# Diagonal blocks of the delta rule by SBUF transfers instead of ACT copies, with the first transpositions and clearings queued behind the last multiplication on DVE

## The chip, the cores and the metric

The kernel runs on one core of a Trainium2 chip. The core has engines that run their own instruction queues in order: PE (TensorE, matrix products; PEld is its weight load), DVE (VectorE), ACT (ScalarE), POOL (GpSimd) and SP (SyncE, which here only issues DMA transfers). The metric is the device time of one execution in microseconds (us), as the median of several executions.

## The reference

One encoder layer in float32 over 1024 tokens of width 1024. Two mixers read the same normalised input through one projection:

```python
xn   = _rmsnorm(h, norm_mix_w[l])
proj = xn @ w_in[l]
q_a, k_a, v_a, qkv_g, z_g, a_g, b_g = jnp.split(proj, SPLIT_POINTS, axis=-1)
attn = _windowed_gqa(...)          # 8 heads, window of 128
gdn  = _gdn_mixer(qkv_g, z_g, ...) # 4 heads of 128, both directions
h = h + jnp.concatenate([attn, gdn], axis=-1) @ w_out[l]
h = h + jnp.square(jax.nn.relu(_rmsnorm(h, norm_ffn_w[l]) @ w_ffn_in[l])) @ w_ffn_out[l]
```

The second mixer is a gated delta rule. In each chunk of tokens it needs the inverse of a unit triangular matrix:

```python
kk    = jnp.einsum("bnhcd,bnhsd->bnhcs", k, k)
a_mat = jnp.where(strict, beta[..., :, None] * kk * decay, 0.0)
t_mat = lax.linalg.triangular_solve(eye + a_mat, eye, left_side=True, lower=True)
```

The change touches only how the small diagonal blocks of `a_mat` are brought together before they are inverted.

## The kernel before

Large products are made in three passes of float32 parts: ACT rounds a weight tile (`split`, L123), POOL subtracts to get the rest (L124), and PE multiplies (L136 to L138 in `mm3`). The rounded weights live in three buffers with the tag `wh`, the rests in three of the tag `wl`, so the two instructions for the next weights can run as soon as PE has released a buffer. Results land in PSUM: four banks have the tag `psA` (the projections), four the tag `psB` (all else).

The stage of the change weaves two streams. The first is the rest of the input projection: v (`proj_conv`), the gate z (`proj_z`, whose results ACT takes out of PSUM with L473) and the attention's keys, values and queries (`proj_attn`, whose results DVE takes out with L491 and L509). The second belongs to the delta rule:

- `prep` loops over 8 chunks of 128 tokens, and in each over the 2 directions. PE makes k by k (`gg`, L646), k by q (`kq`, L648) and the rows of the decay with its mask (`rows`, L653 and L654); ACT takes the exponentials (L658, one for each of 4 heads); DVE multiplies to `at` (L662) and, as the last step, `dec` by `kq` (L670). `at` and `dec` are stored to device memory (L669, L671). ACT copies the four 32x32 diagonal blocks of each head out of `at` into `diag[d]` (L667).
- `eliminate` transposes `diag[d]` in blocks of 32x32 on DVE (L679, once for each direction), clears the result `t` on POOL (L680, L681) and then inverts all 256 blocks at once on DVE, in 31 steps of two instructions (L688, L690), each of which needs the one before.
- `diag_blocks` transposes the inverses back (L699, L700), and `invert` makes the 128x128 inverses from them on PE. It loads `at` again for two chunks (L721, into the buffers of `eliminate`), and begins with the products of L738, followed by L749 and L753.

Who goes first on each engine is set at build time by a scheduler that runs through the program with estimated times; the hardware then follows each queue strictly. `tc.issue_after(i)` puts the instructions of its block, where they are on the engine of instruction `i`, behind `i` in that engine's queue. The heads of v are transposed on PE into `psB` (L424) and multiplied out of it by DVE (L464). SP's queue holds the loads of weights (L254), the stores of `at`, `dec`, z (L474) and v (L465), and the loads of L721. Each transfer names one of eight counters in turn and waits until the eighth transfer before it has landed.

Of the kernel before, what the change touches and what calls it, by code (L numbers as in the profile page):

```python
# [14 lines left out]
ALU = mybir.AluOpType  # L15
# [3 lines left out]
SEQ = 1024  # L19
# [59 lines left out]
class Block:  # L79
# [397 lines left out]
    def proj_attn(self):  # L477


        nc = self.nc  # L480
        w = self.io["w_in"][0]
        raws = self.load_w(self.w_cols(w, C_AK, 256))
        lo, up = slice(0, 64), slice(64, 128)
        self.kh, self.kl = [self.pg(dt=F32R) for _ in range(2)], [self.pg(dt=F32R) for _ in range(2)]
        for v, o in enumerate((up, lo)):
            nc.vector.tensor_copy(out=self.kl[v][o, :], in_=self.zero[o, :].to_broadcast([64, SEQ]))
        self.va = self.pg((P, NT, P))
        for i, half, ps in self.pair(raws):
            tok = slice(half * HALF, (half + 1) * HALF)
            t = self.pt()  # L490
            nc.vector.tensor_copy(out=t, in_=ps)  # L491
            if i == 0:
                swap = self.pt()
                nc.sync.dma_start(out=swap[up, :], in_=t[lo, :])
                nc.sync.dma_start(out=swap[lo, :], in_=t[up, :])
                for v, (r, o) in enumerate(((lo, up), (up, lo))):
                    nc.scalar.copy(out=self.kh[v][r, tok], in_=t[r, :])
                    nc.scalar.copy(out=self.kh[v][o, tok], in_=swap[o, :])
                    nc.gpsimd.tensor_tensor(out=self.kl[v][r, tok], in0=t[r, :], in1=self.kh[v][r, tok].bitcast(F32),
                                            op=ALU.subtract)  # L500
            else:
                pv = self.transposed(t, 0)
                nc.vector.tensor_copy(out=self.va[:, 4 * half:4 * half + 4, :], in_=pv)
            yield 5.2
        for kv in range(2):
            raws = self.load_w(self.w_cols(w, C_AQ + 256 * kv, 256))
            for i, half, ps in self.pair(raws):
                q, qh = self.pt(), self.pt(dt=F32R)
                nc.vector.tensor_scalar(out=q, in0=ps, scalar1=0.125, scalar2=None, op0=ALU.mult)  # L509
                nc.scalar.copy(out=qh, in_=q)  # L510
                nc.gpsimd.tensor_tensor(out=q, in0=q, in1=qh.bitcast(F32), op=ALU.subtract)
                for part, t in enumerate((qh.bitcast(F32), q)):
                    nc.sync.dma_start(out=self.qad[kv, part, i, :, half * HALF:(half + 1) * HALF], in_=t)
                if i == 1 and half == 0:
                    self.qs.append(self.query(0, kv))
                yield 5.2
# [122 lines left out]
    def prep(self):  # L639
        nc = self.nc  # L640
        self.diag = [self.pg((P, 32, 32)) for _ in range(2)]
        for c in range(NT):
            sl = slice(c * P, (c + 1) * P)
            gg, kq = self.ps("psB", (P, GH, P)), self.ps("psB", (P, GH, P))
            for h in range(GH):
                nc.tensor.matmul(gg[:, h, :], self.kT[h][:, sl], self.kT[h][:, sl], start=True, stop=True)  # L646
            for h in range(GH):
                nc.tensor.matmul(kq[:, h, :], self.kT[h][:, sl], self.qT[h][:, sl], start=True, stop=True)  # L648
            for d in range(2):
                dec, at = self.pt((P, GH, P)), self.pt((P, GH, P))  # L650
                rows = self.ps("psB", (P, GH, P))
                i = 2 * c + d
                nc.tensor.matmul(rows, self.selb[:, i:i + 1].to_broadcast([P, P]), self.grow, start=True, stop=False)  # L653
                nc.tensor.matmul(rows, self.identb, self.maskb[d].unsqueeze(1).to_broadcast([P, GH, P]),  # L654
                                 start=False, stop=True)
                for h in range(GH):
                    i = 4 * d + h
                    nc.scalar.activation(out=dec[:, h, :], in_=rows[:, h, :], func=AF.Exp,  # L658
                                         bias=self.ngc[:, c, i:i + 1])
                for h in range(GH):  # L660
                    i = 4 * d + h
                    nc.vector.scalar_tensor_tensor(out=at[:, h, :], in0=dec[:, h, :],  # L662
                                                   scalar=self.cc[:, c, i:i + 1], in1=gg[:, h, :],
                                                   op0=ALU.mult, op1=ALU.mult)
                for q in range(4):
                    r = slice(32 * q, 32 * q + 32)
                    nc.scalar.copy(out=self.diag[d][r, :, 4 * c:4 * c + 4].rearrange("p i h -> p h i"),  # L667
                                   in_=at[r, :, r])
                nc.sync.dma_start(out=self.atd[c, :, d], in_=at)  # L669
                nc.vector.tensor_tensor(out=dec, in0=dec, in1=kq, op=ALU.mult)  # L670
                nc.sync.dma_start(out=self.pd[c, :, d], in_=dec)  # L671
                yield 1.5

    def eliminate(self):

        nc = self.nc
        m, t = self.dbl((P, 2, 32, 32)), self.dbl((P, 2, 32, 32))
        for d in range(2):
            nc.vector.transpose(out=m[:, d].rearrange("p a b -> p b a") if d else m[:, d], in_=self.diag[d])  # L679
        nc.gpsimd.memset(t.rearrange("p d a b -> p (d a b)"), 0.0)  # L680
        nc.gpsimd.memset(t.rearrange("p d a b -> p d (a b)")[:, :, 0:1024:33], 1.0)  # L681
        elim = self.pt((P, 2 * 256))
        yield 1.1
        for k in range(31):
            rr, xx = slice(k + 1, 32), slice(0, k + 1)
            nr, nx = 31 - k, k + 1
            tmp = elim[:, :2 * nr * nx].rearrange("p (d a b) -> p d a b", d=2, a=nr)
            nc.vector.tensor_tensor(out=tmp, in0=m[:, :, rr, k:k + 1].to_broadcast([P, 2, nr, nx]),  # L688
                                    in1=t[:, :, k:k + 1, xx].to_broadcast([P, 2, nr, nx]), op=ALU.mult)
            nc.vector.tensor_tensor(out=t[:, :, rr, xx], in0=t[:, :, rr, xx], in1=tmp, op=ALU.subtract)  # L690
            yield 0.8
        self.tdiag = t
# [745 lines left out]
```

## Time and profile before

| what | value |
|---|---|
| median of 3 runs | 1218.68 us (1217.45 to 1218.98) |
| the profiled execution's own time | 1218.1 us |
| its span, first to last instruction | 1216.4 us |
| mean granted clock of TensorE | 0.99 |
| the stage of the change, `prep` to the first product of `invert` | 147 to 270 us |
| ACT's copies L667 in it | 64, 26.8 us |

The profile is of one execution. A row of a timeline gives start, duration, engine, line and operation, output and inputs by the program's names, a count, and in brackets the idle time before it with what ended it. "SPq" is SP's own queue; its durations include waits between merged instructions. The tables by windows give the busy time of PE, PEld, DVE, ACT and POOL, then the granted clock (1.00 is full speed), the share of the DMA engines and GB/s.

### The profile page before, as it was taken

What the parts mean: (1) busy time and instruction counts of PE and PEld (TensorE: products, weight loads), DVE (VectorE), ACT (ScalarE), POOL (GpSimd) and SP (SyncE); (2) the same over time, 40 slices, a digit from 0 to 9 for tenths busy, and PEclk for the clock granted to TensorE, in tenths of its full rate; (3) what the DMA queues carried; (4) which work ended last, traced back from release to release, by engine and by line L of the source; (5) the groups of instructions that cost most, each with busy time, mean ns of one, the idle gap of its engine ahead of it and who ended that gap; (6) DMA issues with size and microseconds to landing.
All of it is one profiled execution on the core that took longest, in us unless ns stands there. A gap on an engine that the chain in (4) does not pass through costs nothing. (4 is left out here: it accounts for less than half of the span.)

```text
span 1216.4 us, 18458 instructions
## 1 busy us (share of the span) xinstructions
PE 1172.0 (96%) x6482; PEld 960.5 (79%) x6482; DVE 855.4 (70%) x1482; ACT 610.8 (50%) x1331; POOL 559.8 (46%) x470
## 2 busy tenths in 40 slices
PE   6999999899979999999999999999999999999996
PEld 5788878687768778888788888888878888888875
DVE  4676667994489996687854445454599796987976
ACT  6455597425385762134755454454645444334443
POOL 5354211234421224143855453544546565555694
PEclk9999999899989999999999999999999999999999
DMA  6124344433635667323153444444779535443323
GB/s 246 48 95 146 93 163 165 165 130 112 206 122 184 187 212 265 126 91 122 54 176 121 160 149 156 140 153 140 251 278 327 183 104 177 135 156 104 104 87 139
DMA packets 121630, 187.62 MB, mean 154 GB/s; under 512 B 11044, under 2 KB 64417, under 8 KB 121538
## 3 DMA queue, kind: packets, MB, share of 16 engines
q1 hardware_dynamic: 103876, 155.20, 38.7%
q10 hardware_dynamic: 17661, 31.24, 6.8%
q8 instruction: 51, 0.84, 0.3%
q14 instruction: 42, 0.34, 0.1%
HBM read 122.39 MB, written 63.49 MB: 153 GB/s over the span
## 5 line engine op out<-in xcount | busy, mean ns | idle before, releaser
L136 PE MATMUL psA<-pg,wh 128*128 128x512 f32 x416 | 165.2, 398 | 2.1 <-ACT pt L473 2.1
L138 PE MATMUL psA<-pg,wl 128*128 128x512 f32 x416 | 164.5, 395 | 0.0
L137 PE MATMUL psA<-pg,wh 128*128 128x512 f32 x416 | 164.2, 395 | 0.0
L124 POOL TENSOR_TENSOR wl<-wr,wh 128x512 fp32r<-128x512 f32 x44 | 66.3, 1529 | 156.8 <-ACT wh L123 129.0
L1207 DVE TENSOR_TENSOR pg<-pg 128x512 fp32r<-128x512 f32 x112 | 125.1, 1151 | 12.1 <-ACT pg L1206 12.1
L124 POOL TENSOR_TENSOR wh<-wr,wh 128x512 fp32r<-128x512 f32 x32 | 47.6, 1507 | 139.5 <-ACT wh L123 139.5
L1124 ACT ACTIVATE pt<-pt 128x512 f32<-128x512 f32 x64 | 40.4, 632 | 119.2 <-DVE pt L1114 114.7
L137 PE MATMUL psA<-pg,pg 128*128 128x512 f32 x256 | 99.6, 391 | 0.3 <-POOL pg L124 0.2
L136 PE MATMUL psA<-pg,pg 128*128 128x512 f32 x256 | 98.7, 390 | 0.9 <-DVE pg L1252 0.9
L138 PE MATMUL psA<-pg,pg 128*128 128x512 f32 x256 | 99.2, 389 | 0.0
L136 PEld LDWEIGHTS psA<-pg,wh 128*128 128x128 f32 x416 | 78.8, 189 | 19.5 <-ACT pt L473 2.4
L137 PEld LDWEIGHTS psA<-pg,wh 128*128 128x128 f32 x416 | 78.9, 190 | 18.0 <-issue 0.9
L138 PEld LDWEIGHTS psA<-pg,wl 128*128 128x128 f32 x416 | 78.8, 189 | 16.8
L124 POOL TENSOR_TENSOR pg<-wr,pg 128x512 fp32r<-128x512 f32 x48 | 73.7, 1567 | 39.3 <-ACT pg L123 39.3
L1206 ACT CAST pg<-pg 128x512 fp32r<-128x512 f32 x112 | 66.9, 620 | 37.6 <-DMA pg<-sd 27.8
L137 PE MATMUL psB<-pg,pg 128*128 128x512 f32 x192 | 74.9, 390 | 0.8 <-POOL pg L124 0.7
L138 PE MATMUL psB<-pg,pg 128*128 128x512 f32 x192 | 74.7, 389 | 0.0
L136 PE MATMUL psB<-pg,pg 128*128 128x512 f32 x192 | 74.7, 389 | 0.0
L123 ACT CAST wh<-wr 128x512 fp32r<-128x512 f32 x76 | 43.6, 623 | 52.7 <-PE psA L137 32.0
L1114 DVE TENSOR_TENSOR pt<-psB,pt 128x512 f32<-128x512 f32 x39 | 26.9, 689 | 58.8 <-PE psB L138 40.1
L1114 DVE TENSOR_TENSOR pt<-psA,pt 128x512 f32<-128x512 f32 x39 | 26.8, 688 | 52.6 <-PE psA L138 35.2
L136 PEld LDWEIGHTS psA<-pg,pg 128*128 128x128 f32 x256 | 48.0, 188 | 12.3 <-DVE pg L1252 2.2
(395 smaller groups left out, 3231.4 us busy)
## 6 DMA issues: line engine op xcount, KB each, us to landing
sd<-pt ACTq DMA_DIRECT2D x112, 256.0 KB, 2.0
pg<-sd SPq DMA_DIRECT2D x112, 256.0 KB, 2.9
wr<-in_w_ffn_in SPq DMA_DIRECT2D x32, 512.0 KB, 3.6
wr<-in_w_in SPq DMA_DIRECT2D x22, 512.0 KB, 3.9
pg<-in_x SPq DMA_DIRECT2D x16, 512.0 KB, 5.0
wr<-in_w_ffn_out SPq DMA_DIRECT2D x16, 512.0 KB, 4.6
sc<-kvd SPq DMA_DIRECT2D x14, 512.0 KB, 4.7
kvd<-pt SPq DMA_DIRECT2D x16, 256.0 KB, 2.4
```

What stands on the lines that cost most here:

```text
L123: a = nc.scalar.copy(out=h, in_=raw)
L124: b = (eng or nc.gpsimd).tensor_tensor(out=l, in0=raw, in1=h.bitcast(F32), op=ALU.subtract)
L136: nc.tensor.matmul(ps, wh, xh, start=first, stop=False, skip_group_check=onto)
L137: nc.tensor.matmul(ps, wh, xl, start=False, stop=False, skip_group_check=onto)
L138: return nc.tensor.matmul(ps, wl, xh, start=False, stop=last, skip_group_check=onto)
L1114: self.nc.vector.tensor_tensor(out=out, in0=in0, in1=in1, op=ALU.add)
L1124: self.nc.scalar.activation(out=c, in_=c, func=AF.Relu)
L1206: nc.scalar.copy(out=s[:, 0], in_=raw)
L1207: v.tensor_tensor(out=s[:, 1], in0=raw, in1=s[:, 0].bitcast(F32), op=ALU.subtract)
```

## The change

Three things. The four ACT copies for each chunk and direction become four DMA transfers from `at` to `diag[d]` within SBUF, issued by SP behind the store of `at`; each moves 32 partitions with four pieces of 128 bytes. `diag[d]` is now laid out with the blocks outside and the columns inside, so that a piece is contiguous, and the transpositions read it with a stride. Last, the two transpositions, and two clearings of `proj_attn` that also run on DVE (L486), are queued behind the last L670.

```diff
@@ proj_attn
-        for v, o in enumerate((up, lo)):
-            nc.vector.tensor_copy(out=self.kl[v][o, :], in_=self.zero[o, :].to_broadcast([64, SEQ]))
+        with self.tc.issue_after(self.decayed):
+            for v, o in enumerate((up, lo)):
+                nc.vector.tensor_copy(out=self.kl[v][o, :], in_=self.zero[o, :].to_broadcast([64, SEQ]))
@@ prep
+                nc.sync.dma_start(out=self.atd[c, :, d], in_=at)
                 for q in range(4):
                     r = slice(32 * q, 32 * q + 32)
-                    nc.scalar.copy(out=self.diag[d][r, :, 4 * c:4 * c + 4].rearrange("p i h -> p h i"),
-                                   in_=at[r, :, r])
-                nc.sync.dma_start(out=self.atd[c, :, d], in_=at)
-                nc.vector.tensor_tensor(out=dec, in0=dec, in1=kq, op=ALU.mult)
+                    nc.sync.dma_start(out=self.diag[d][r, 4 * c:4 * c + 4, :], in_=at[r, :, r])
+                self.decayed = nc.vector.tensor_tensor(out=dec, in0=dec, in1=kq, op=ALU.mult).ins
@@ eliminate
-        for d in range(2):
-            nc.vector.transpose(out=m[:, d].rearrange("p a b -> p b a") if d else m[:, d], in_=self.diag[d])
+        with self.tc.issue_after(self.decayed):
+            for d in range(2):
+                nc.vector.transpose(out=m[:, d].rearrange("p a b -> p b a") if d else m[:, d],
+                                    in_=self.diag[d].rearrange("p x i -> p i x"))
```

The scheduler moves other instructions with it, nearly all of them between 150 and 224 us; behind that the queues stand as before but for a few neighbours that change places in the attention. In the pieces below, the lines of the changed kernel are one higher than before from L486 on, two higher from L680 on, L663 is the former L662, L666 stores `at` and L669 are the new transfers.

ACT at the end of `prep`: chunk 6 ends and chunk 7 (`pt_1859`, `pt_1905`) follows; `wh_2224` and `wh_2450` are weights of the gate's second half and of the attention's keys. Before:

```order
L658 ACTIVATE pt_1829<-psB_1831,ngc 128x128 x4
L667 COPY pg_1290<-pt_1810 32x4x32 x4
L123 CAST wh_2224<-wr_2178 128x512
L123 CAST wh_2224<-wr_2180 128x512
L667 COPY pg_1291<-pt_1830 32x4x32 x4
L658 ACTIVATE pt_1859<-psB_1861,ngc 128x128 x4
L658 ACTIVATE pt_1905<-psB_1907,ngc 128x128 x4
L667 COPY pg_1290<-pt_1860 32x4x32 x4
L123 CAST wh_2450<-wr_2439 128x512
L123 CAST wh_2450<-wr_2441 128x512
L667 COPY pg_1291<-pt_1906 32x4x32 x4
L473 ACT_TABLE_LOAD
```

and with the change:

```order
L659 ACTIVATE pt_1829<-psB_1831,ngc 128x128 x4
L123 CAST wh_2224<-wr_2178 128x512
L123 CAST wh_2224<-wr_2180 128x512
L659 ACTIVATE pt_1859<-psB_1861,ngc 128x128 x4
L659 ACTIVATE pt_1905<-psB_1907,ngc 128x128 x4
L123 CAST wh_2450<-wr_2439 128x512
L123 CAST wh_2450<-wr_2441 128x512
L473 ACT_TABLE_LOAD
```

The copies are gone and the rest keeps its order, up to the first L473 that empties a bank of the gate.

DVE at the same place (`pg_1290` and `pg_1291` are `diag[0]` and `diag[1]`, `pg_2445` and `pg_2446` are cleared for the attention's keys). Before:

```order
L486 CAST pg_2445<-zero 64x1024
L486 CAST pg_2446<-zero 64x1024
L662 SCALAR_TENSOR_TENSOR pt_1860<-pt_1859,cc,psB_1849 128x128 x4
L662 SCALAR_TENSOR_TENSOR pt_1906<-pt_1905,cc,psB_1849 128x128
L670 TENSOR_TENSOR pt_1859<-pt_1859,psB_1850 128x512
L662 SCALAR_TENSOR_TENSOR pt_1906<-pt_1905,cc,psB_1849 128x128 x3
L679 STREAM_TRANSPOSE dbl_1925<-pg_1290 128x1024
L670 TENSOR_TENSOR pt_1905<-pt_1905,psB_1850 128x512
L679 STREAM_TRANSPOSE dbl_1925<-pg_1291 128x32x32
L688 TENSOR_TENSOR pt_1931<-dbl_1925,dbl_1926 128x62
```

and with the change:

```order
L663 SCALAR_TENSOR_TENSOR pt_1860<-pt_1859,cc,psB_1849 128x128 x4
L663 SCALAR_TENSOR_TENSOR pt_1906<-pt_1905,cc,psB_1849 128x128
L670 TENSOR_TENSOR pt_1859<-pt_1859,psB_1850 128x512
L663 SCALAR_TENSOR_TENSOR pt_1906<-pt_1905,cc,psB_1849 128x128 x3
L670 TENSOR_TENSOR pt_1905<-pt_1905,psB_1850 128x512
L487 CAST pg_2445<-zero 64x1024
L487 CAST pg_2446<-zero 64x1024
L680 STREAM_TRANSPOSE dbl_1925<-pg_1290 128x1024
L680 STREAM_TRANSPOSE dbl_1925<-pg_1291 128x32x32
L690 TENSOR_TENSOR pt_1931<-dbl_1925,dbl_1926 128x62
```

The last L670 no longer stands behind a transposition, and the clearings moved from ahead of chunk 7 to between L670 and the transpositions. On POOL, the clearing of `t` moved behind the two L124 of `wl_2451`.

SP at the end of `prep`. Before:

```order
L254 DMA wr_2793<-in_w_in 128x4x256
L254 DMA wr_2795<-in_w_in 128x4x256
L669 DMA atd<-pt_1860 128x512
L671 DMA pd<-pt_1859 128x512
L669 DMA atd<-pt_1906 128x512
L671 DMA pd<-pt_1905 128x512
```

and with the change:

```order
L666 DMA atd<-pt_1860 128x512
L669 DMA pg_1290<-pt_1860 32x4x32 x4
L671 DMA pd<-pt_1859 128x512
L666 DMA atd<-pt_1906 128x512
L669 DMA pg_1291<-pt_1906 32x4x32 x4
L671 DMA pd<-pt_1905 128x512
L254 DMA wr_2793<-in_w_in 128x4x256
L254 DMA wr_2795<-in_w_in 128x4x256
```

The gathers stand between the stores, and the two weight loads moved behind all of `prep`.

## The prediction

> **What bounds the kernel now.** I read the page first, then PE's timeline between 205 and 276 us, where all of the change lies, then the timelines of ACT, DVE, POOL and SP beside it and the granted clock in windows of 1 us.
>
> ```profile
> PE 1172.0 (96%) x6482; PEld 960.5 (79%) x6482; DVE 855.4 (70%) x1482; ACT 610.8 (50%) x1331; POOL 559.8 (46%) x470
> ```
>
> PE is busy for 96% of the span, so only what moves PE's idle time or its clock counts. One of its holes is here:
>
> ```profile
> 215.82 0.66 PE L424 MATMUL psB<-ident,sc 128*128 128x128 f32 x4 [0.17 <-ACT pt L658]
> 220.21 0.66 PE L424 MATMUL psB<-ident,sc 128*128 128x128 f32 x4 [1.72 <-DVE pt L670]
> 223.01 0.79 PE L136 MATMUL psA<-pg,wh 128*128 128x512 f32 x1 [2.15 <-ACT pt L473]
> ```
>
> The v heads' transpositions (L424) wait for PSUM that the last chunk of the preparation holds, and the gate's second half (L136) waits until ACT has emptied a bank (L473). Between 215.6 and 223.0 PE does four groups of 0.66 us. The clock follows; the columns after the window are PE, PEld, DVE, ACT, POOL, then PEclk:
>
> ```profile
> 218.00:219.00 1.00, 0.49 (x4) 0.25 (x3) 0.67 (x1) 0.98 (x3) 0.00 (x0) 1.00 0.88 187
> 222.00:223.00 1.00, 0.00 (x0) 0.00 (x0) 1.00 (x1) 0.99 (x3) 0.00 (x0) 0.50 0.54 207
> 228.00:229.00 1.00, 1.00 (x5) 0.77 (x4) 0.93 (x3) 0.00 (x0) 0.00 (x0) 0.60 1.15 385
> 229.00:230.00 1.00, 1.00 (x6) 0.83 (x5) 0.93 (x3) 0.00 (x0) 0.00 (x0) 1.00 1.04 399
> ```
>
> From 223.0 to 228.8 PE works at half clock, 2.9 us lost. ACT is the cause of the hole, and the copies that the change takes away (L667) are what fills it:
>
> ```profile
> 214.62 2.17 ACT L658 ACTIVATE pt<-psB,ngc 128x128 f32<-128x128 f32 x8
> 216.63 1.67 ACT L667 COPY pg<-pt 32x128 f32<-32x128 f32 x4
> 218.33 1.14 ACT L123 CAST wh<-wr 128x512 fp32r<-128x512 f32 x2
> 219.37 1.68 ACT L667 COPY pg<-pt 32x128 f32<-32x128 f32 x4
> 221.07 1.28 ACT L473 ACT_TABLE_LOAD   x1
> ```
>
> But a second chain runs beside PE: the elimination on DVE (L688 and L690), the transposed blocks (L699, L700), and then the inversion's first product on PE (L738).
>
> ```profile
> 221.08 1.93 DVE L679 STREAM_TRANSPOSE dbl<-pg 128x1024 f32<-128x1024 f32 x1 [0.93 <-ACT pg L667]
> 223.10 0.26 DVE L688 TENSOR_TENSOR pt<-dbl,dbl 128x62 f32<-128x62 f32 x1
> 262.12 1.25 DVE L699 STREAM_TRANSPOSE sc<-dbl 128x1024 f32<-128x1024 f32 x1
> 263.29 2.08 DVE L700 STREAM_TRANSPOSE sc<-dbl 128x1024 f32<-128x1024 f32 x1
> 265.30 1.19 DVE L699 STREAM_TRANSPOSE sc<-dbl 128x1024 f32<-128x1024 f32 x1
> 270.12 0.69 DVE L491 COPY pt<-psA 128x512 f32<-128x512 f32 x1
> ```
> ```profile
> 269.44 1.09 PE L738 MATMUL psB<-sc,dbl 32*32 32x32 f32 x64
> 271.02 0.22 PE L749 MATMUL psB<-sc,pt 32*32 32x32 f32 x1 [0.49 <-ACT pt L741]
> 272.24 0.50 PE L136 MATMUL psA<-pg,wh 128*128 128x512 f32 x1
> ```
> ```profile
> 275.00:330.00 55.00, 54.05 (x607) 44.23 (x607) 19.90 (x46) 21.17 (x36) 24.59 (x24) 1.00 0.50 160
> ```
> ```profile
> 261.89 7.52 SPq L721 DMA_DIRECT2D dbl<-atd  x4
> dbl<-atd SPq DMA_DIRECT2D x4, 512.0 KB, 4.9
> ```
>
> L738 needs two loads (L721) that are issued when the elimination has left their buffer, 261.89; the second, some 0.4 us behind, lands 4.9 us later at 267.2. PE came at 269.44, so the slack is 2.2 us. L136 at 272.24 needs the bank that L491 empties by 270.81: slack 1.4 us. From 275 to 330 us PE is busy for 54.05 of 55, and ACT and DVE follow it there, so **the time of L136 at 272.24 is what the change moves**, and it can come at most 1.4 us earlier, however fast PE gets there, unless DVE's chain is earlier as well.
>
> **The change part by part.**
>
> *What PE gains before 262 us.* The 64 copies go:
>
> ```profile
> L667 ACT COPY pg<-pt x64: 397/418/437, 148.9 to 220.6; 32x128 f32<-32x128 f32 x64
> L669 SPq DMA_DIRECT2D atd<-pt x16: 319/320/502, 150.7 to 217.8; - x16
> DMA to landing us min/median/max: 2.0/2.0/5.6
> L486 DVE CAST pg<-zero x2: 691/1170/1650, 212.3 to 213.0; 64x1024 fp32r<-64x1024 f32 x2
> 216.92 0.85 DVE L662 SCALAR_TENSOR_TENSOR pt<-pt,cc,psB 128x128 f32<-128x128 f32 x3
> 213.00 0.38 PE L654 MATMUL psB<-maskb,identb 128*128 128x512 bf16 x1
> ```
>
> That is 26.8 us of ACT, most of it hidden. The last exponentials (L658) then start when PE's mask product is there: 213.4, less the two matmuls that the new order puts behind it (six start in the microsecond at 229, so 0.4), about 213.0 in place of 214.62. DVE's last three L662 ended 217.77, 3.15 us behind L658's start; so they now end at 216.0 at the latest, I take 215.7, and L670 (0.65, the next on DVE but for the transposition) at 216.4. No L424 waits long. On ACT, the split L123 can start when the gate's fourth product ends, 215.7, then 1.14, the table load 1.28, one L473 at 0.6: PE restarts at 218.9 instead of 223.0, after a pause under 2 us. The row at 218 shows the clock still whole after a stretch about as thin, so I count the 2.9 us too. **PE's lead: 4.1 + 2.9 = 7.0 us**; it would reach L738 at 262.4.
>
> *When the elimination starts.* DVE's order is now L670, the two clearings L486 (0.69 + 1.65 = 2.3 us with POOL beside the second, as in the row; 1.4 without), transposition, transposition. The transfers: SP issues the tile's own store and four gathers, 5 x 0.32 us, after the last L662 at 215.7, so the last goes out near 217.3 and lands at 219.3 with the row's 2.0 (222.9 with its 5.6). No row shows pieces of 128 bytes; the median of 2.0 is the nearest. The first transposition starts at 216.4 + 2.3 = 218.7 and now reads with a stride. L700, which does that, takes 2.08 where L699 takes 1.25, so 2.1. The second strides on both sides: 2.0 (the longer of 1.93 and 2.08) to 2.8 (1.25 with both surcharges). So L688 starts between 222.8 and 223.6, near 221.9 with unhindered clearings and 224.5 with both hindered; I take 223.4, **0.3 us later than before**. DVE gains nothing, because what ACT gave up is paid in strides and in a landing.
>
> *What the earlier PE triggers.* ACT and POOL split the next weights as soon as PE has released a buffer, so L123 and L124 move with PE. L124 on POOL slows the elimination:
>
> ```profile
> 242.82 0.69 DVE L690 TENSOR_TENSOR dbl<-dbl,pt 128x512 f32<-128x512 f32 x1
> 243.54 1.67 DVE L688 TENSOR_TENSOR pt<-dbl,dbl 128x510 f32<-128x510 f32 x1
> 245.24 1.66 DVE L690 TENSOR_TENSOR dbl<-dbl,pt 128x510 f32<-128x510 f32 x1
> 243.16 3.19 POOL L124 TENSOR_TENSOR wl<-wr,wh 128x512 fp32r<-128x512 f32 x2 [21.48 <-ACT wh L123]
> 264.63 2.55 POOL L124 TENSOR_TENSOR wl<-wr,wh 128x512 fp32r<-128x512 f32 x2 [16.08 <-ACT wh L123]
> 270.07 2.51 POOL L124 TENSOR_TENSOR wl<-wr,wh 128x512 fp32r<-128x512 f32 x2 [2.89 <-ACT wh L123]
> ```
>
> Each POOL instruction costs one DVE instruction 0.98 us, a pair 1.96. One pair falls into the elimination before. The pair at 264.63 fell behind it (262.1) and moves to 257.6: in. The pair at 270.07 moves to 263.1; with the second pair the elimination lasts until 262.1 + 0.3 + 1.96 = 264.3, so that one is in too (bounds 0 and 1.96). **The chain ends 0.3 + 3.9 = 4.2 us later.**
>
> The Trainium skill, "SBUF — State Buffer", section on SBUF's two separate sides, says that VectorE and GpSimd share one port pair, locked for a whole instruction, against a VectorE instruction with two SBUF inputs only if GpSimd reads SBUF. The trace agrees with the blocking. A whole POOL instruction of 1.25 in place of 0.98 would add 1.1 us to the sum by this page.
>
> *Where it comes out.* The loads land at 267.2 + 4.2 = 271.4. PE has then stood for 9 us and is at half clock, as after 222. What small products do there:
>
> ```profile
> 338.00:339.00 1.00, 1.00 (x24) 1.00 (x23) 0.00 (x0) 1.00 (x6) 0.52 (x1) 0.50 0.00 0
> 337.61 1.94 PE L774 MATMUL psB<-pt,dbl 64*64 64x64 f32 x30 [0.82 <-issue]
> 357.08 1.14 PE L774 MATMUL psB<-pt,dbl 64*64 64x64 f32 x30
> ```
>
> A factor of 1.7: L738 1.85, then 0.5 for ACT's copy, L749 and L753 1.2 x 1.7 = 2.1. L136 at 271.4 + 4.45 = 275.85 (L491 is done at 275.0). The clock came back 5.8 us after the restart at 223.0; here that is 277.2, which costs half of 1.35, 0.7 (0 to 1.7). So 276.5 against 272.24, **4.3 us later**. Later swaps of order near 355 and 366 us move PE by a score product or two: 0, give or take 0.4.
>
> Sum: the profiled execution's 1218.1 (its span 1216.4 and 1.7 around it) + 4.3 = 1222.4. The median of the runs is 1218.68, so I write 1222.5. By the clearings, the second stride, the third pair and the clock, the forecast's own range is 1220.2 to 1225.
>
> **The rivals.**
>
> *Little change: the third pair misses.* If the chain starts by 222.5, or PE's lead is smaller, the pair moved from 270.07 meets its last instructions at most, and then the transpositions; these POOL leaves alone: L699 took 1.19 at 265.30 beside the pair of 264.63, and 1.25 at 262.12 without. With a start 0.6 us earlier than before and one pair more: L738 at 267.2 + 1.4 = 268.6, L136 at 273.0, with the clock 273.7: +1.5 us, 1219.6; it spans 1218 to 1221. For it: the clearings may run unhindered. Against it: L123 on ACT now frees POOL at just that time.
>
> The Trainium skill, "TensorE: Matmul & The Clock Gate", Part 1, puts the throttle behind an idle window of about 3.4 us; here it came at 222.0 although PE had run 0.66 us since 218.6. By either, the new pause of under 2 us should keep the clock. Were it lost, the lead is about 4 us and this rival holds, 1219 to 1221.
>
> *The transfers are late.* SP now issues 96 instead of 32 transfers in this stage, in order, and each waits for the eighth before it. If the gathers land after 5.6 us or the pieces of 128 bytes are slow, the elimination starts 2 us later still: 1224.5 to 1226. For it: two loads of 512 KB share the queue. Against: these now stand behind the last gather, and 2.0 is the median.
>
> *Faster: the chain starts early and POOL does not meet it.* It decides at L688: if it starts by 221 (clearings 1.4, transpositions 1.25 and 1.93, transfers at 2.0) and the pairs cost the small late instructions of the chain next to nothing, L738 is at 265.2, PE stands under 3.4 us at full clock, and L136 follows L491 at 268.8: 3.4 us gained, 1214.7. For it: only the longest L688 were seen beside POOL. Against: L700's stride.
>
> *The copies were not the cause* would leave the hole at 216 to 223 and 1218. Against it: ACT has no idle time there; it is part of the second case.
>
> **How the numbers follow.** Forecast 0.48; little change 0.26; late transfers 0.13; faster 0.13. Within 0.2% (2.4 us, what this kernel's runs can tell) of 1218.7 lie 1216.3 to 1221.1: most of the second case and a little of the first and the last. So faster 0.12, same 0.27, slower 0.61. The range 1217 to 1225.8 leaves out most of the last case and the far end of the third.
>
> **What would show it.** Right: no wait for L473 of 2 us and clock 1.00 after 220; L688 first near 223.4; two more pairs of L688/L690 stretched by 1 us near 258 and 263; a PE wait of about 9 us for the loads before L738, with the clock at 0.5 behind it. Wrong: L738 earlier than 269.4, the elimination shorter than 41 us, or a first transposition that waits for transfers beyond 221.

## The result, and the profile after

| | before | after |
|---|---|---|
| median | 1218.2 us (1217.45 to 1218.98) | 1225.98 us (1223.67 to 1227.01) |
| ratio to before, 95% interval | | 1.0059 (1.0046 to 1.0072) |
| the profiled execution, its span | 1218.1 us, 1216.4 us | 1225.58 us, 1223.9 us |

The changed kernel is slower by 0.6%. Of the lines of its code used below, L659 is L658 of before, L680 the first transpositions (L679), L690 and L692 the elimination (L688, L690), L701 and L702 the transpositions back (L699, L700), L723 the loads (L721), L740 and L751 the first products of `invert` (L738, L749), L487 and L492 the clearings and the copies that empty the AK banks (L486, L491). AK and AQ stand for the projections of the attention's keys, with its values, and of its queries.

PE's timeline, after:

```profile
214.71 2.11 PE L424 MATMUL psB<-ident,sc 128*128 128x128 f32 x16
217.84 0.50 PE L136 MATMUL psA<-pg,wh 128*128 128x512 f32 x1 [1.01 <-ACT pt L473]
...
273.12 0.28 PE L740 MATMUL psB<-sc,dbl 32*32 32x32 f32 x2 [11.47 <-DMA dbl<-atd]
274.58 1.11 PE L740 MATMUL psB<-sc,dbl 32*32 32x32 f32 x62 [1.18 <-DMA dbl<-atd]
...
278.32 0.79 PE L136 MATMUL psA<-pg,wh 128*128 128x512 f32 x1 [0.86 <-DVE pt L492]
...
288.01 1.15 PE L784 MATMUL psB<-pg,pt 64*64 64x64 f32 x32 [0.69 <-ACT pt L778]
```

The hole at 216 to 223 us is gone: the four groups of L424 run in one piece, and the gate's product restarts at 217.84 where it stood at 223.01. And a larger hole has come: 11.5 us in which PE waits for the loads of `invert`. Windows of the same trace, with the granted clock behind POOL's column:

```profile
222.00:223.00 1.00, 1.00 (x6) 0.80 (x6) 0.95 (x1) 0.00 (x0) 0.00 (x0) 1.00 0.11 17
...
262.54:265.95 3.41, 0.00 (x0) 0.00 (x0) 3.31 (x4) 0.12 (x1) 3.25 (x4) 1.00 0.00 0
265.95:269.37 3.42, 0.00 (x0) 0.00 (x0) 3.11 (x10) 0.00 (x0) 0.00 (x0) 0.50 0.00 0
276.20:279.61 3.41, 2.55 (x99) 2.23 (x100) 3.31 (x8) 3.33 (x6) 0.00 (x0) 0.50 0.79 261
279.61:283.02 3.41, 3.41 (x9) 2.64 (x9) 1.74 (x4) 3.34 (x6) 1.04 (x1) 0.50 0.37 129
283.02:286.43 3.41, 3.41 (x22) 2.57 (x23) 0.00 (x0) 0.66 (x2) 3.01 (x5) 1.00 0.00 0
```

The clock is whole at 222, drops to half in the stop at 265.95 and is whole again only at 283.0. The same PE instructions in both traces give the account of the time:

| instruction on PE (before's line) | before | after | later by |
|---|---|---|---|
| gate's product, L136 | 223.01 | 217.84 | -5.2 |
| the AK products at 259.4, L137 | 259.38 | 251.52 | -7.9 |
| first product of `invert`, L738 | 269.44 | 273.12 | +3.7 |
| second, L749 | 271.02 | 276.15 | +5.1 |
| L136 behind them | 272.24 | 278.32 | +6.1 |
| L782 | 279.78 | 288.01 | +8.2 |
| end of the span | 1216.4 | 1223.9 | +7.5 |

PE's lead was real, and the loss stands complete by 288 us. The chain on DVE that PE then waited for:

```profile
216.14 4.55 DVE L487 CAST pg<-zero 64x1024 fp32r<-64x1024 f32 x2
220.86 2.10 DVE L680 STREAM_TRANSPOSE dbl<-pg 128x1024 f32<-128x1024 f32 x1 [0.16 <-issue]
224.52 2.21 DVE L680 STREAM_TRANSPOSE dbl<-pg 128x1024 f32<-128x1024 f32 x1 [1.56 <-DMA pg<-pt]
226.83 0.27 DVE L690 TENSOR_TENSOR pt<-dbl,dbl 128x62 f32<-128x62 f32 x1
...
257.06 1.59 DVE L692 TENSOR_TENSOR dbl<-dbl,pt 128x440 f32<-128x440 f32 x1
...
264.15 1.42 DVE L690 TENSOR_TENSOR pt<-dbl,dbl 128x312 f32<-128x312 f32 x1
...
269.83 1.25 DVE L701 STREAM_TRANSPOSE sc<-dbl 128x1024 f32<-128x1024 f32 x1
277.57 0.69 DVE L492 COPY pt<-psA 128x512 f32<-128x512 f32 x1
```

It starts at 226.83 (223.10 before) and lasts 43.0 us (39.0 before). The second transposition waits for a transfer. SP's queue beside it, and the gathers' group (duration of one issue on SP: least, median, most):

```profile
216.04 0.37 SPq L666 DMA_DIRECT2D atd<-pt  x1
216.76 2.53 SPq L669 DMA_DIRECT2D pg<-pt  x4
219.40 0.52 SPq L671 DMA_DIRECT2D pd<-pt  x1
220.02 0.38 SPq L666 DMA_DIRECT2D atd<-pt  x1
220.45 2.54 SPq L669 DMA_DIRECT2D pg<-pt  x4
```
```profile
L669 SPq DMA_DIRECT2D pg<-pt x64: 589/599/1449, 151.3 to 222.4; - x64
DMA to landing us min/median/max: 1.8/1.9/5.2
```

A gather costs SP 0.60 us, against 0.32 for a whole store before; the two stores themselves take 0.38 and 0.52 us here. A set of a store, four gathers and a store takes 3.7 to 4.0 us, and the last sets stand back to back from 204 us on: the tile whose decays were ready at 215.4 is served last, and SP starts to issue its fourth gather at 222.4. The landing (1.9) is as quick as any.

POOL's pairs, which were at 264.63 and 270.07 and are now inside the elimination:

```profile
256.77 3.03 POOL L124 TENSOR_TENSOR wl<-wr,wh 128x512 fp32r<-128x512 f32 x2 [16.08 <-ACT wh L123]
262.22 3.02 POOL L124 TENSOR_TENSOR wl<-wr,wh 128x512 fp32r<-128x512 f32 x2 [2.41 <-ACT wh L123]
```

### The profile page after: what moved, and what is told of

Read it like the earlier page. It is cut to its first block, busy times and chain, and to the rows that moved or that the text cites. A ratio compares the mean times of both kernels' runs of the same rounds, so it can differ in the third digit from the quotient of the medians.

```text
span 1223.9 us, 18507 instructions
## 1 busy us (share of the span) xinstructions
PE 1170.8 (96%) x6482; PEld 960.9 (79%) x6482; DVE 865.4 (71%) x1482; ACT 585.0 (48%) x1267; POOL 559.6 (46%) x470
## 5 line engine op out<-in xcount | busy, mean ns | idle before, releaser
L136 PE MATMUL psA<-pg,wh 128*128 128x512 f32 x416 | 165.0, 397 | 1.9 <-ACT pt L473 1.0
L137 PE MATMUL psA<-pg,wh 128*128 128x512 f32 x416 | 164.4, 395 | 0.0
L124 POOL TENSOR_TENSOR wl<-wr,wh 128x512 fp32r<-128x512 f32 x44 | 66.2, 1525 | 149.1 <-ACT wh L123 135.3
L124 POOL TENSOR_TENSOR wh<-wr,wh 128x512 fp32r<-128x512 f32 x32 | 47.4, 1499 | 139.6 <-ACT wh L123 139.6
L136 PE MATMUL psA<-pg,pg 128*128 128x512 f32 x256 | 98.7, 390 | 0.9 <-DVE pg L1254 0.9
L137 PE MATMUL psA<-pg,pg 128*128 128x512 f32 x256 | 99.1, 390 | 0.0
L136 PEld LDWEIGHTS psA<-pg,wh 128*128 128x128 f32 x416 | 78.7, 189 | 19.2 <-ACT pt L473 1.3
L137 PEld LDWEIGHTS psA<-pg,wh 128*128 128x128 f32 x416 | 78.7, 189 | 18.0 <-issue 0.9
L124 POOL TENSOR_TENSOR pg<-wr,pg 128x512 fp32r<-128x512 f32 x48 | 74.1, 1575 | 38.2 <-ACT pg L123 38.2
L137 PE MATMUL psB<-pg,pg 128*128 128x512 f32 x192 | 74.9, 390 | 0.8 <-POOL pg L124 0.7
L136 PE MATMUL psB<-pg,pg 128*128 128x512 f32 x192 | 74.7, 389 | 0.0
L136 PEld LDWEIGHTS psA<-pg,pg 128*128 128x128 f32 x256 | 48.1, 188 | 12.2 <-DVE pg L1254 2.2
```

Source lines behind the costliest of these rows:

```text
L124: b = (eng or nc.gpsimd).tensor_tensor(out=l, in0=raw, in1=h.bitcast(F32), op=ALU.subtract)
L136: nc.tensor.matmul(ps, wh, xh, start=first, stop=False, skip_group_check=onto)
L137: nc.tensor.matmul(ps, wh, xl, start=False, stop=False, skip_group_check=onto)
```

## The experiments

My theory: the copies' removal gives PE its lead; what sets the end is DVE's chain, which starts later (SP's queue) and is longer (two more POOL pairs); and the stop that follows costs clock as well. The rivals: the clearings' place is the cause; the transfers alone; the order alone; the lead is not real. In the rows of a run the line numbers are those of its own kernel, up to some ten lines further on; the operation and the tiles tell which instruction it is.

| run | what | median us | ratio to before, 95% |
|---|---|---|---|
| 1 | order part alone | 1223.93 | 1.0044 (1.0029 to 1.0059) |
| 2 | gathers alone | 1227.47 | 1.0063 (1.0042 to 1.0083) |
| 3 | changed, POOL held behind the elimination | 1221.82 | 1.0023 (1.0013 to 1.0034) |
| 4 | changed, other work in PE's stop | 1230.23 | 1.0096 (1.0081 to 1.0111) |
| 5 | the same, loads behind the swaps | 1217.89 | 0.9991 (0.9980 to 1.0003) |
| 6 | gathers alone, last chunk by ACT copies | 1215.83 | 0.9977 (0.9963 to 0.9991) |
| 7 | run 6, POOL held | 1218.28 | 0.9994 (0.9981 to 1.0008) |
| 8 | before, other work as in run 5 | 1216.97 | 0.9985 (0.9972 to 0.9997) |
| 9 | run 6, PE kept busy near 331 us | 1219.59 | 1.0008 (0.9996 to 1.0020) |
| 10 | run 6, AK banks emptied by ACT | 1217.59 | 0.9991 (0.9978 to 1.0004) |
| 11 | 9 and 10 together | 1218.95 | 1.0007 (0.9996 to 1.0018) |
| 12 | run 1 again | 1223.49 | 1.0038 (1.0024 to 1.0052) |

### Where the late start comes from: runs 2 and 6

Run 2 is the changed kernel with both `issue_after` blocks taken away:

```diff
-        with self.tc.issue_after(self.decayed):
+        with contextlib.nullcontext():
             for v, o in enumerate((up, lo)):
                 nc.vector.tensor_copy(out=self.kl[v][o, :], ...)
...
-        with self.tc.issue_after(self.decayed):
+        with contextlib.nullcontext():
             for d in range(2):
                 nc.vector.transpose(...)
```

> The gathers and the strided transpositions are kept, the clearings are free to go earlier; the order puts them ahead of the last two groups of decays, where DVE was idle from 208.2 to 212.6 us in the changed kernel. My theory (SP's queue is the bound: six sets of one store, four gathers and one store stand back to back, 3.7 us each, and the last gather goes out at 222.9): the first transposition starts some 2 us earlier at most, the second still waits until 224.4, first elimination step 226.5 to 226.9, time 1225 to 1226. Rival (the clearings' 4.55 us are the cause): first elimination step at 222 to 223.5, time 1221 to 1222.

DVE's timeline of run 2:

```profile
210.78 1.41 DVE L487 CAST pg<-zero 64x1024 fp32r<-64x1024 f32 x2 [2.84 <-PE psB L649]
...
220.63 2.09 DVE L680 STREAM_TRANSPOSE dbl<-pg 128x1024 f32<-128x1024 f32 x1 [4.81 <-DMA pg<-pt]
224.29 2.19 DVE L680 STREAM_TRANSPOSE dbl<-pg 128x1024 f32<-128x1024 f32 x1 [1.57 <-DMA pg<-pt]
226.58 0.27 DVE L690 TENSOR_TENSOR pt<-dbl,dbl 128x62 f32<-128x62 f32 x1
```

The clearings now cost 1.41 us in a gap where DVE had nothing to do, and the elimination starts at 226.58 instead of 226.83. The first transposition waits 4.81 us for gathers. So the clearings, for all their 4.55 us in the changed kernel, cost next to nothing there: they stood inside the wait for SP. The median, 1227.47, lies 1.5 us above the range named, on four runs from 1224.67 to 1229.91; with that spread run 2 can't be told from the changed kernel.

Run 6 takes run 2 and lets ACT copy the last chunk, so that SP has eight gathers fewer:

```diff
-                    nc.sync.dma_start(out=self.diag[d][r, 4 * c:4 * c + 4, :], in_=at[r, :, r])
+                    if c < NT - 1:
+                        nc.sync.dma_start(out=self.diag[d][r, 4 * c:4 * c + 4, :], in_=at[r, :, r])
+                    else:
+                        nc.scalar.copy(out=self.diag[d][r, 4 * c:4 * c + 4, :], in_=at[r, :, r])
```

(For the last chunk the store of `at` goes behind the copies.)

> Gathers for the first seven chunks, copies on ACT for the last one; clearings free to go early, as in the second run of this study (first elimination step at 226.6). My theory (the start is set by SP's backlog): the last gather goes out near 215.5, the last copy ends at 217.7, the first elimination step is at 222.0 to 222.8, 4 us earlier; PE pays for it with 3.3 us of its restart (221), and its clock may fall there; time 1217 to 1220. Rival (the strided transpositions and the landing set the start, not the queue): first step at 225 or later, time 1224 and more.

SP's last gathers, ACT's copies, the first transposition and the first step on DVE, POOL's pair, DVE's copies ahead of the first AK bank, and PE's wait in run 6:

```profile
211.82 2.63 SPq L671 DMA_DIRECT2D pg<-pt  x4
...
214.28 1.22 ACT L673 COPY pg<-pt 32x128 f32<-32x128 f32 x4 [0.83 <-DVE pt L663]
...
215.80 1.95 DVE L686 STREAM_TRANSPOSE dbl<-pg 128x1024 f32<-128x1024 f32 x1
...
220.41 0.26 DVE L696 TENSOR_TENSOR pt<-dbl,dbl 128x62 f32<-128x62 f32 x1
...
260.71 2.55 POOL L124 TENSOR_TENSOR wl<-wr,wh 128x512 fp32r<-128x512 f32 x2 [16.08 <-ACT wh L123]
...
265.83 3.76 DVE L739 COPY pg<-sc 32x256 f32<-32x256 f32 x4
...
270.37 0.50 PE L136 MATMUL psA<-pg,wh 128*128 128x512 f32 x1 [2.02 <-DVE pt L492]
```

The start comes 6.2 us earlier than in run 2, and earlier than the 222.0 to 222.8 expected. The last copy ended at 217.8, as expected, but the first transposition had run ahead of it, at 215.80, and only the second stood behind it. The elimination lasts 39.0 us and ends at 259.41, before POOL's pair at 260.71. SP's queue is the cause of the late start. Against the changed kernel this is 0.8% faster (1215.83 against 1225.98); against before by 0.23%, and below the 1217 to 1220 expected.

PE restarts at 219.74, with the clock at half until 224.2, and still comes to `invert` 3.9 us earlier than in before without a wait. It loses 2.0 of that to the first AK bank. The chain ended 2.7 us earlier than in before, yet the copy that empties the bank starts only 0.5 earlier (269.63 against 270.12): DVE's four copies ahead of it take 3.76 us beside POOL's next pair, at 266.16. In before they ended as that pair began, at 270.07:

```profile
268.51 1.58 DVE L731 COPY pg<-sc 32x256 f32<-32x256 f32 x4
```

In runs 6, 7 and 9 to 12, with the pair beside them, these copies take 3.67 to 3.79 us; in before, the changed kernel and runs 2 and 3, without it, 1.58 to 1.73. No run holds this pair back, so the link is read from these traces alone.

### What POOL's pairs cost: runs 3 and 7

In run 3 the subtractions for the first AQ weights stand behind a POOL instruction of one element that reads the last row of the elimination:

```diff
+            with self.behind(self.gate):
                 self.split(view(raws[kh]), h[:, 4 * kh:4 * kh + 4, :], l[:, 4 * kh:4 * kh + 4, :])
...
+                last = self.tdiag[:, 0, 31, 0:1]
+                g = nc.gpsimd.tensor_tensor(out=self.small((P, 1)), in0=last, in1=last, op=ALU.subtract)
+                self.gate = [g.ins]
```

> The changed kernel with POOL's subtractions for the first AQ weights held behind a tiny POOL instruction that reads the last row of the elimination, so that the pairs at 256.8 and 262.2 us cannot meet it. My theory (each pair costs the chain 1.95 us and the chain sets the end): no stretched instructions after 240, the elimination ends at 265.9 instead of 269.8, the first product of the inversion starts 3.9 earlier, at 269.2, time 1221 to 1222. Rival (the late transfers alone make the loss, the pairs are hidden behind the loads): the product starts at 272 to 273 and the time is 1225.

POOL and PE in run 3:

```profile
265.59 4.96 POOL L124 TENSOR_TENSOR wl<-wr,wh 128x512 fp32r<-128x512 f32 x4
...
268.65 0.28 PE L747 MATMUL psB<-sc,dbl 32*32 32x32 f32 x2 [7.27 <-DMA dbl<-atd]
```

The elimination goes from 226.35 to 265.36, 39.0 us, and PE's stop shrinks from 11.5 to 7.3 us. The median falls by 4.2 us (1225.98 to 1221.82). The pairs cost what the theory said, and the rival falls.

Run 7 is run 6 with the same hold.

> The same with POOL's two pairs held behind the elimination. My theory (start and collisions are the two terms of the chain, and they add): the elimination takes 39.0 us as before and ends at 261 to 262, PE reaches the inversion at 265 to 268 and waits 0 to 2 us; 1216 to 1218.5, no slower than before. Rival (any lead of PE that ends in a wait costs more by the clock than it brings): 1219 to 1221.

It gave 1218.28, 0.9994 of before, within the theory's range by 0.2 us: with the late start and the two pairs both taken out, the loss is gone, and no gain is left. In run 6 the pair already came 1.3 us behind the elimination, so the hold had nothing to add; what differs between the traces of 6 and 7 is the clock, below.

### Is the lead worth anything: runs 4, 5 and 8

Run 4: ACT instead of DVE empties the AK banks (L492), the inversion is emitted later, and its first product stands behind the second AQ tile.

```diff
-            nc.vector.tensor_copy(out=t, in_=ps)
+            nc.scalar.copy(out=t, in_=ps)
...
+    def pause(self):
+        yield 23
...
+                        with self.behind([self.gemmed] if i == 0 else []):
                             nc.tensor.matmul(px[blk(e), n, :], at[d][blk(s), n, blk(e)], ...)
```

> The changed kernel, but PE has other work in its stop: ACT instead of DVE empties the banks of the AK products, and the inversion is queued behind the second AQ tile, some 11 us of products later. My theory (the lead of 7.9 us is real and is lost only because PE waits for the chain): PE does the two tiles in what was its stop, waits 0 to 4 us for the first product of the inversion, the clock stays whole, 1210 to 1215 us. Rival (the end of the elimination sets the time, whatever PE does meanwhile): 1222 to 1226. Rival (the lead isn't real): 1218.

It was 1230.23, slower than all. SP and PE in run 4:

```profile
272.72 0.89 SPq L727 DMA_DIRECT2D dbl<-atd  x2
273.70 0.47 SPq L496 DMA_DIRECT2D pt<-pt  x1
...
280.82 1.12 PE L425 MATMUL psB<-ident,pt 128*128 128x128 f32 x4 [13.94 <-ACT pt L493]
```

The loads of `invert`, which wait for the elimination, had been queued on SP ahead of a swap (L496) that ACT needs; behind ACT's wait stood the next bank, behind that PE. None of the expectations was tested.

Run 5 queues the loads behind the last swap and the inversion behind three AQ tiles; run 8 does the same to before.

```diff
+                with self.behind([self.swapped] if i == 0 else []):
                     nc.sync.dma_start(out=a, in_=self.atd[2 * i:2 * i + 2, :, d]...)
```

> As the kernel before this in the study (ACT empties the AK banks, the inversion stands behind AQ tiles), mended: in that one the loads for the inversion stood on SP ahead of the swaps that fill the second half of the AK tiles, so ACT and then PE waited 14 us for the end of the elimination all the same. Here these loads are queued behind the last swap, and the inversion behind three AQ tiles (16.4 us of PE). My theory (the lead is real and lost only in the wait for the chain): PE works without a stop of more than 2 us from 218 to 278, at clock 1.00, and is 6 to 8 us ahead of before behind it: 1210 to 1213 us. Rival (what the inversion delivers is needed by then, so the loss comes back at the scan): 1217 to 1224.

> Control: the same shift of work as in the fifth run (ACT empties the AK banks, inversion behind three AQ tiles), made in the kernel before. My theory: before has no stop there that the shift could fill, its hole at 216 to 223 stays: 1216 to 1219. Rival (the shift of work is itself a gain, whatever the copies): as the fifth run within 2 us.

PE in run 5, a window and a later row:

```profile
262.00:278.00 16.00, 15.99 (x73) 12.91 (x71) 15.28 (x24) 0.68 (x2) 3.92 (x3) 1.00 0.14 48
...
326.00:346.00 20.00, 11.90 (x144) 10.04 (x146) 14.41 (x45) 14.31 (x39) 5.24 (x5) 0.66 0.43 138
```
```profile
335.66 0.44 PE L782 MATMUL psB<-pt,dbl 64*64 64x64 f32 x2 [3.34 <-DVE pt L773]
```

PE works through its former stop, 15.99 of 16 us, at whole clock. The attention's eight score products of 128x256, which start at 325.92 to 329.19 in before, still start at 319.29 to 325.01 there, at least 4.2 us earlier. By 353 us PE is 0.2 us later than before: waits for DVE and a transfer near 330, and half clock from 328.6 to 342.2, have taken it. The median is 1217.89, that of run 8 (which keeps the hole at 216 to 223) 1216.97; run 8 lies in the ranges of both its theories and decides nothing between them. The rival of run 5 was right: what the change wins for PE is worth nothing here even when no stop follows at once, since a later wait takes it.

### The order alone and the clock: runs 1, 9 to 12

Run 1 puts ACT's copies and the old layout back and keeps the two `issue_after` blocks; run 12 repeats it.

> The copies on ACT are back; of the change only the order on DVE is kept (clearings and both transpositions behind the last multiplication). My theory (the lead comes from the copies' removal, the loss from a later chain on DVE): PE's hole at 216 to 223 us and its half clock return; the two clearings stand between the last multiplication and the second transposition, 2.4 to 4.6 us long, partly inside the wait for ACT's copies, so the first elimination step starts 1 to 3 us later than before's 223.1. Before has 2.2 us of slack on the chain's end: 1218 to 1220. Rival (the order alone is what costs): the elimination starts at 226 or later and the time is 1222 or more.

> The order part alone once more, for more executions: it came out at 1223.9 in four runs, where 1218 to 1220 was expected. Its trace shows 2.25 us lost in this stage (chain 1.9 later, clock at half for 3.4 us), and 3 more at three clock drops near 440, 600 and 904, where before had one. Theory (whether a short pause of PE halves the clock depends on how it falls on windows that run freely, so those are luck): 1220 to 1222. Rival (the order itself costs 5): 1223 to 1225.

PE and two windows in run 12:

```profile
273.76 0.79 PE L136 MATMUL psA<-pg,wh 128*128 128x512 f32 x1 [1.91 <-DVE pt L492]
```
```profile
269.14:272.55 3.41, 2.17 (x148) 1.76 (x136) 3.35 (x4) 3.28 (x7) 3.10 (x4) 1.00 0.62 204
272.55:275.97 3.42, 2.21 (x5) 1.82 (x6) 3.30 (x9) 3.34 (x6) 0.28 (x1) 0.50 0.56 171
```

The theory missed in both: 5 us slower, not 0 to 2 or 2 to 4, and the repetition kept it, so luck with the clock's windows is not the whole reason. The times are those of the rival, that the order alone costs this, but the start of the elimination that it named for run 1 (226 or later) did not come. So the order alone makes the kernel slower by 0.4%, the gathers alone by 0.6%, and both together by 0.6%: the two don't add, and the changed kernel doesn't need the order for its loss.

In run 1 the chain starts 0.8 us later (clearings between the transpositions, 3.00 us) and its last step meets a POOL pair (1.26 instead of 0.22), so the copy that empties the first AK bank starts at 272.20 instead of 270.12. In run 12 it is the copies ahead of the bank that meet a pair (3.71 us from 269.28, the pair at 269.39), and the bank's copy starts at 273.02. PE waits 1.5 us for it there (1.9 in run 12), where before had no wait. That, with the small products ahead of it, leaves PE busy for 2.17 of 3.41 us in run 12, and the clock is half in what follows. In run 12 L136 is 1.5 us late by the wait and the work 4.1 us behind the clock; in run 1 it is 0.7 and 2.25. What is left to the 5 us comes later and isn't accounted for. Before has no wait at this place:

```profile
269.76:273.17 3.41, 2.92 (x156) 2.57 (x145) 1.76 (x4) 3.28 (x7) 3.04 (x4) 1.00 0.99 342
```

It stood close to this edge: a bank 2 us later is enough for the wait and the clock.

Runs 6, 7 and 9 to 11 share this place. Windows of run 7 and run 6:

```profile
266.13:269.55 3.42, 2.28 (x161) 2.01 (x160) 3.38 (x4) 3.29 (x7) 2.84 (x3) 1.00 0.64 195
269.55:272.96 3.41, 2.39 (x6) 1.91 (x7) 3.28 (x8) 3.32 (x6) 0.45 (x2) 0.50 0.60 186
```
```profile
268.52:271.93 3.41, 1.56 (x7) 1.30 (x8) 3.31 (x8) 3.34 (x6) 0.87 (x3) 1.00 0.58 199
271.93:275.34 3.41, 3.41 (x16) 2.57 (x14) 1.48 (x3) 2.71 (x5) 2.28 (x2) 1.00 0.22 50
```

Nearly the same pause (1.7 and 2.0 us before L136) halved the clock in run 7 and not in run 6, where it fell differently on the windows. I take this to be why the relatives of run 6 lie between 0.9977 and 1.0008; it is argued from single traces, not shown. So run 6 beats the changed kernel, and that it beats before by more than this luck is not settled.

Run 9 adds to run 6 fourteen products that nobody reads, ahead of the wait near 331 us; run 10 gives the AK banks and the swaps' issue to ACT; run 11 has both.

```diff
+            if i == 2:
+                idle = self.ps("psB", (P, GH, P))
+                for _ in range(14):
+                    nc.tensor.matmul(idle, self.identb, self.maskb[0].unsqueeze(1).to_broadcast([P, GH, P]),
+                                     start=True, stop=True)
             px = self.ps("psB", (P, 8, 64))
```

> The kernel with the last chunk copied on ACT (gathers for the others), plus 14 products of 128x512 whose result nobody reads, put ahead of the product of the second inversion that waits 4.0 us for ACT near 331 us (L774 in before). Clock theory (a window of 3.41 us in which PE is busy for less than about half is followed by half clock): the clock stays 1.00 from 330 to 344, where it was 0.50 for 10 us, and PE is 2 to 3 us earlier behind it: 1212.5 to 1214. Rival (the work there waits for ACT and DVE anyway, so the slower clock costs nothing): 1215.8, as without.

> The kernel with the last chunk copied on ACT, where PE's lead of 3.9 us shrank to 1.9 in a wait of 2.0 us for DVE's copy of the first AK bank (L491 in before). Here ACT empties the AK banks, and the swaps are issued by ACT, not behind SP's loads. Theory: no such wait, PE keeps 3.9 us: 1213.5 to 1214.5. Rival (the lead is taken back in the wait for ACT near 331 us, which sits on DVE's and ACT's chain): 1215.5 to 1216.

> Both of the two before. If they are independent they add: 1211 to 1212.5. If the wait near 331 us takes back what the AK banks give, it is as the first of them: 1213 to 1214.

In run 9 the clock stays whole until 341.3 and the 30 products take 1.11 us instead of 1.94, yet PE is 1.27 us behind before at the start of this stretch (327.30 against 326.03) and at its end (341.49 against 340.22): after the products it waits for DVE (1.50 where run 6 waited 0.68). Here the slow clock costs nothing that DVE's chain doesn't cost anyway. In run 10 the wait did not go; ACT and PE there:

```profile
268.62 2.64 ACT L771 COPY pt<-sc 32x256 f32<-32x256 f32 x4
...
271.93 0.79 PE L136 MATMUL psA<-pg,wh 128*128 128x512 f32 x1 [1.87 <-ACT pt L492]
```

The scheduler put the first bank behind ACT's copies L771, and PE waited 1.87 us for ACT in place of 2.02 for DVE. Both theories had assumed the wait away, so run 10 tells nothing of them, and run 11 only repeats 9. The medians of runs 9, 10 and 11 (1219.59, 1217.59 and 1218.95) lie above every range named for them.

## Why the prediction was right, and where its size was off

*What bounds the kernel* was right: the time of L136 at 272.24 is what moved, and all of the loss is there by 288 us.

*PE's lead* was right: 7.9 us against 7.0, clock whole, restart at 217.84 against 218.9 (the terms shown add up to 218.7).

*The start of the elimination* is the step that failed: 226.83 against 223.4. "SP issues the tile's own store and four gathers, 5 x 0.32 us, after the last L662 at 215.7, so the last goes out near 217.3": I priced a gather by the store's row, and counted the last tile alone on an empty queue. A gather takes 0.60 us to issue, a set 3.7 to 4.0, and the queue was behind since 204 us; the issue of the last began at 222.4. The landing (1.9 against 2.0) and the strided transpositions (2.10 and 2.21 against 2.1 and 2.0 to 2.8) were right. The clearings were mis-sized too (4.55 against 2.3, POOL beside both). Run 2 shows that this cost next to nothing behind SP's queue; without the queue it would have shown, since 220.7 with 2.1 and 2.2 for the transpositions gives 225.0, an estimate from the rows above.

*The pairs* were right: two more inside, at 256.8 and 262.2 (257.6 and 263.1), and 43.0 us of elimination where 39.0 + 3.9 were summed; run 3 takes them out and gets 4.2 us back. The Trainium skill, "SBUF — State Buffer", section on SBUF's two separate sides, has the port pair locked for the whole instruction, which made 1.1 us more. The stretch was 0.94 to 0.97 us for each POOL instruction of these two pairs (1.59 less the 0.62 of its neighbour), though each of them took 1.5 us: the measurement decides for the row's price.

*Where it comes out*: L136 was put at 275.85, and with the start 3.4 us later at 279.25; it came at 278.32, 0.9 us sooner, and by another path. The loads let the bulk of L740 start at 274.58, 0.2 before the 274.8 that the sum then gives. The factor of 1.7, read off products of 64x64, did not hold for those of 32x32: at half clock 62 of them took 1.11 us, where 64 took 1.09 at whole clock in before, and L751 with its neighbours 1.31 against 1.29. So PE was ready for L136 at 277.46, and waited 0.86 us for the AK bank, which DVE emptied by 278.26 (the prediction's 275.0, and 3.4). The bank at the end of DVE's chain set L136, not the loads. The clock was mis-sized: back "5.8 us after the restart", cost 0.7. It came back at 283.0, 9.9 us after the restart, and cost 2.15 (from +6.08 to +8.23), because the groups of small products with waits between them did not bring it back (the window at 276.20, 2.55 of 3.41 us busy, was followed by half clock), and the first window of PE busy throughout did. Later differences gave 0.7 back, a little more than the term of 0.4.

So 4.3 forecast and 7.5 measured: 3.4 more from SP's queue, 1.45 more from the clock, 0.9 less up to L136 and 0.7 less later. The median, 1225.98, lies 0.2 us above the range, and 1 us above the forecast's own.

*The rivals.* The measured time lies in the range of "the transfers are late", and its first words, 96 transfers in order where 32 were, are the mechanism. Its conditions were not: no slow landing, no slow pieces, but the time that SP itself takes to issue. "Little change" and "faster" both needed a start by 222.5 or 221; run 6 has one (220.41) and comes out between them. "The copies were not the cause" falls with the row at 217.84.

*What would make it wrong* named "a first transposition that waits for transfers beyond 221". It was the second that waited, to 224.52.

## What to carry to other kernels

A transfer's price is not only its landing: its issue takes the queue, and many small transfers in place of copies must be summed on that queue from the first one that falls behind. A lead on the bounding engine is worth what is left of it at the next wait; look for the chain that sets that wait, and for what the lead sets free to collide with it. Where that engine stands near the edge of the clock's windows, a short wait may cost more than itself (run 12: L136 1.5 us late, the work behind it 4.1), and the runs of one kernel may differ by as much (run 6: 1212.72 to 1219.49).

## What the runs showed of the hardware

- Issuing a gather of 32 partitions with four pieces of 128 bytes took SP 0.60 us (median of 64), a store of 128 x 512 took 0.32 (before), and 0.38 and 0.52 us with gathers in the queue. ACT's copy of the same block took 0.42 us into the strided layout and 0.30 into the contiguous one, so on the engine that issues, the gather was dearer than the copy.
- In each of the traces the clock changes at times that are multiples of 3.41 us apart (before: 221.97, 228.80, 334.61, 344.85), and their offset differs between executions (265.95 in after is no such multiple from 221.97). The Trainium skill, "TensorE: Matmul & The Clock Gate", Part 1, section "What's actually happening", has a window of 3413 ns that runs freely; the traces agree. The same page's section on oscillation warns of idle gaps over some 3.4 us. Here a gap of 1.9 us among small products was enough (2.17 of 3.41 us busy, run 12); the measurement decides. What share of a window keeps the clock is not settled: 1.56 busy kept it in run 6 and 2.28 lost it in run 7, the latter mostly 32x32 products.
- At half clock 62 products of 32x32 took 1.11 us (after, 274.58), where 64 took 1.09 at whole clock (before, 269.44); 30 of 64x64 took 1.94 against 1.11 (runs 6 and 9).
- Two clearings of 64x1024 on DVE took 1.41 us by themselves and 4.55 with POOL's subtractions and clearing beside them. Four copies of 32x256 took 1.58 us by themselves and 3.76 with a pair of POOL's subtractions beside them (before and run 6).
